# Hybrid encoder layer: VectorE held to the written order in the convolution stage, with its norm dealt out between matmul pieces

## The chip, the cores and the metric

The kernel runs on one core of a Trainium2 chip. The metric is the device time of one execution in microseconds (us); three runs of the kernel before gave 1720.52, 1720.84 and 1724.67, with a median of 1720.84. Profiles are of one execution each. The engines are TensorE (PE: matmuls, with PEld for its weight loads), VectorE (DVE), ScalarE (ACT), GpSimd (POOL) and SyncE (SP, which issues most transfers).

## What is computed

One layer of an encoder on a sequence of 1024 positions with width 1024, all in float32. The part that matters here is the token mixer:

```
h    = rmsnorm(x)
proj = h @ w_in                       # 1024 x 8192: glu (2x512), q, v, z_f, z_b, og, g_a, g_b
a    = glu(proj[glu])                 # 512 channels
a    = depthwise_conv(a, 31 taps) + b
a    = silu(layernorm(a) * ln_w + ln_b)
a    = a @ pw_w                       # 512 -> 1024
o    = bidirectional gated scan over q, v, z_f, z_b
y    = sigmoid(g_a) * a + sigmoid(g_b) * (norm(o) * silu(og)) @ o_w
x    = x + y @ w_out
```

A feed-forward block with a gated three-tap convolution and a last norm follow.

## The kernel before

**Layout.** Channels lie on the 128 partitions and positions along the free axis, in two halves of 512 (`H`). Every matrix product is made of 128 x 128 x 512 matmuls. For precision an operand is split into a high and a low part, and each product is three matmuls (`mm3`, lines 148 to 150). `split` (line 124) makes the parts: ScalarE casts the high part into its page, then VectorE subtracts it from the source and writes the low part.

**Pairs.** Most columns of the combined projection are made two column blocks at a time by `pair_job`, with Strassen's scheme in Winograd's form: seven products instead of eight, in the order 1, 2, 6, 7, 5, 4, 3. One product is twelve matmuls, in two pieces of six; a pair has 14 pieces, and there are 19 pairs (`NPAIRS`), so 266 pieces. Products 1, 6, 5 and 3 add up in one bank `mm` (the row bank), product 2 goes into `tr`, 7 and 4 into `sc`. Copies of a bank to SBUF are ScalarE's (line 440). VectorE evacuates three of the four quadrants through `store` (line 817): evac(0,0) after product 2, evac(1,1) after product 5, evac(1,0) after product 4; evac(0,1), after product 3, is ScalarE's. Product 3 adds into the row bank that evac(1,1) reads, so it waits for that evacuation.

The weights of a pair are three wide pages (1024 elements a partition) and a half one, each as high and low part: one for products 1 and 2 and one for 6 and 3 (both from the ring `wp`, four pages), one for 7 and 5 and the half page for 4 (ring `wq`, three pages). They are made from loaded rows (ring `wr`, two pages), a column page (`sw`) and a quadrant (`w4`). Sums of weight blocks come either from VectorE (`first`, pair 0 and from pair 14 on) or from accumulating transfers that GpSimd issues (line 301).

**Order.** `run_jobs` takes a job's pieces one by one and prepares the next job after `lead` pieces of the current one. `Weights` holds the preparation as steps with pauses in between; each piece advances it by one tick. Without `late` all steps of a pair are run at once when it is prepared. `Stream.fill(n)` issues n pieces, keeping fractions. TensorE's instructions keep the written order in the whole kernel (`tc.manual_schedule` with PE alone, at the top). The other engines' instructions are put in order by the compiler's scheduler, except those that `pin` ties behind what was written before them on their engine.

**The convolution stage.** `conv_steps` (lines 1042 to 1058) is four channel groups of 31 taps, one VectorE instruction of 128 x 1024 each (lines 1050 and 1053), 124 in all; after each, 1.67 pieces of the pairs are issued (`CONV_FILL`). A group's result is stored to the DRAM scratch `d_cv` in two halves. For each half of the positions the layer norm follows in lumps: load the four groups back, issue 6 pieces, sum them and have TensorE add over the partitions (`all_rows`, line 591, a product with ones), subtract the mean (line 1081), issue 6 pieces, squares on ScalarE, sums on VectorE, one-column products for the sum of squares (line 602), 1/sqrt on GpSimd, 5 pieces, spread over the partitions again, then scale, shift, silu, split, store to `d_ca`, 12 pieces. `s_pairs.drain()` issues the rest. The scan's stage follows, with the remaining projections as filler.

The feed-forward block, much later, runs pairs as well, with `late=True`, no `direct`, and `lead` 1.

Of the kernel before, what the change touches and what calls it, by code (L numbers as in the profile page):

```python
# [10 lines left out]
F32 = mybir.dt.float32  # L11
F32R = mybir.dt.float32r
I32 = mybir.dt.int32
U8 = mybir.dt.uint8
AF = mybir.ActivationFunctionType
ALU = mybir.AluOpType
AX = mybir.AxisListType

P = 128
FILL = 1.77  # L20
TAIL = ((1, 2), (1, 1), (2, 4), (2, 3))
CONV_FILL = 1.67
NPAIRS = 19
LN_FILL = 6
LN_LAST = 12
GLU_FIRST = 4
GLU_LEAD = 6
GLU_FILL = 2
# [3 lines left out]
H = 512  # L32
# [15 lines left out]
def tile_hybrid_encoder(  # L48
# [22 lines left out]
    nc = tc.nc  # L71
    PSUM = bass.MemoryType.PSUM
    V, A, G, T = nc.vector, nc.scalar, nc.gpsimd, nc.tensor

    S, D = x.shape[1], x.shape[2]
    ND = D // P
    CW = conv_dw_w.shape[2]
    CK = conv_dw_w.shape[1]
    NCW = CW // P
# [6 lines left out]
    cp = ctx.enter_context(tc.tile_pool(name="const", bufs=1))  # L86
# [7 lines left out]
    def nm(s):  # L94
        uid[0] += 1
        return f"{s}_{uid[0]}"
# [3 lines left out]
    def bank(tag):  # L100
        return ps.tile([P, H], F32, tag=tag, name=nm(tag), bufs=BANKS[tag])

    def page(pool, tag, bufs, dt=F32):
        return pool.tile([P, H], dt, tag=tag, name=nm(tag), bufs=bufs)

    def tmp():
        return page(mp, "tm", 4)
# [15 lines left out]
    def split(hi, lo, src, eng, late=False):  # L123
        parts = A.copy(hi, src), eng.tensor_tensor(lo, src, hi.bitcast(F32), op=ALU.subtract)  # L124
        if late:
            for i in parts:
                pin(i)
        return hi, lo
# [65 lines left out]
    def run_jobs(jobs, lead=0, prime=0, first=None):  # L194


        live = collections.deque(maxlen=3)

        jobs = jobs if isinstance(jobs, collections.deque) else collections.deque(jobs)
        ready = collections.deque()  # L200

        def prepare(n):
            while jobs and len(ready) < n:
                prep, run = jobs.popleft()
                ready.append((run, prep()))
                live.append(ready[-1][1])

        def tick():
            for w in live:
                if isinstance(w, Weights):  # L210
                    w.tick()
            advance_chores()

        prepare(max(prime, 1))
        if prime:
            yield
        while ready:
            run, w = ready.popleft()
            pieces = run(w)
            for _ in itertools.islice(pieces, lead if first is None else first):  # L220
                tick()
                yield
            first = None
            prepare(1)
            for _ in pieces:
                tick()
                yield
            prepare(1)
# [299 lines left out]
    def vec(key, i):  # L528
        name, o = vec_off[key]
        return vecs[name][:, o + i : o + i + 1]  # L530


    def scratch(name, *dims):
        if not dims:
            return dp.tile([P, H], F32, name=name)
        return [scratch(f"{name}_{i}", *dims[1:]) for i in range(dims[0])]

    d_h = scratch("d_h", ND // 2)
    d_c = scratch("d_c", ND // 2, 4)
    d_cv = scratch("d_cv", NCW, 2)  # L540
    d_ca = scratch("d_ca", NCW, 2, 2)
    d_a = scratch("d_a", ND, 2)
    d_ga = scratch("d_ga", ND, 2)
# [29 lines left out]
    def rstd_small(dst, ss, n, late=False):  # L573
        hold = pin if late else lambda i: i
        hold(G.tensor_scalar(dst, ss, 1.0 / n, EPS, op0=ALU.mult, op1=ALU.add))
        hold(G.tensor_tensor(dst, dst, mhalf.to_broadcast(list(dst.shape)), op=ALU.pow))

    def diagonals(r):

        tiny = [cp.tile([P, 4], F32R, name=nm("rp"), tag=tag, bufs=2) for tag in ("rh", "rl")]  # L580
        split(*tiny, r, V)
        pages = [page(mp, "tm", 4, F32R) for _ in range(2)]
        for d, t in zip(pages, tiny):
            for c in range(4):
                gain = t.bitcast(F32)[:, c : c + 1]
                A.activation(d[:, c * P : (c + 1) * P], ident, AF.Copy, scale=gain)
        return pages

    def all_rows(b, parts):
        for n, part in enumerate(parts):  # L590
            T.matmul(b, ones_r, part, start=n == 0, stop=n == len(parts) - 1)
        return b

    def spread(b, rs, diags):
        A.copy(rs, all_rows(b, diags))
        return rs

    def rstd_over_partitions(sq, n, tag, rs, early=False):

        b = bank(tag)  # L600
        for c in range(4):
            T.matmul(
                b[:, c : c + 1], sq[:, c * P : (c + 1) * P], ones_m[:, 0:1], start=True, stop=True
            )
        r = cp.tile([P, 4], F32, name=nm("r4"), tag="r4", bufs=2)
        V.tensor_copy(r, b[:, 0:4])
        rstd_small(r, r, n, early)
        if early:
            diag = tmp()
            pin(  # L610
                G.tensor_tensor(
                    diag.rearrange("p (c e) -> p c e", c=4),
                    view(ident, 0, [[0, 4], [1, P]]),
                    view(r, 0, [[1, 4], [0, P]]),
                    op=ALU.mult,
                )
            )
        else:
            diags = diagonals(r)
        yield  # L620
        b = bank(tag)
        if early:
            T.matmul(b, ones_m, diag, start=True, stop=True)
            pin(A.copy(rs, b))
            yield rs
        else:
            yield spread(b, rs, diags)
# [178 lines left out]
    gl = []  # L806
# [40 lines left out]
    def in_pair(n):  # L847
        (c0, e0), (c1, e1) = todo[2 * n], todo[2 * n + 1]
        evs = (e0, e1)
        return pair_job(  # L850
            in_cols(c0),
            in_cols(c1),
            NK2,
            lambda i: ht[i],
            p1,
            p1,
            lambda e, *quadrant: evs[e](*quadrant),
            first=n == 0 or n >= 14,
            columns=2,
        )  # L860

# [175 lines left out]

    jobs = collections.deque(in_pair(n) for n in range(1, NPAIRS))
    jobs.appendleft((lambda: w_pair0, pair0[1]))
    s_pairs = Stream(run_jobs(jobs, 4))  # L1040

    def conv_steps():
        for j in (3, 0, 1, 2):
            acc = p1.tile([P, S], F32, tag="ca", name=nm("acc"), bufs=2)
            g = gl[j]

            def tap(k):
                return vec("cdw", k * NCW + j)

            V.tensor_scalar(acc, g[:, 0:S], tap(0), vec("cb", j), op0=ALU.mult, op1=ALU.add)  # L1050
            yield
            for k in range(1, CK):
                V.scalar_tensor_tensor(  # L1053
                    acc, g[:, k : k + S], tap(k), acc, op0=ALU.mult, op1=ALU.add
                )
                yield
            for half in range(2):
                nc.sync.dma_start(d_cv[j][half], acc[:, half * H : (half + 1) * H])

    for _ in conv_steps():  # L1060
        s_pairs.fill(CONV_FILL)


    def total(ts, o):
        V.tensor_tensor(o, ts[0], ts[1], op=ALU.add)
        for t in ts[2:]:
            V.tensor_tensor(o, o, t, op=ALU.add)
        return o

    for half in range(2):  # L1070
        xs = []
        for j in range(NCW):
            if j % 2 == 0:
                both = p1.tile([P, 2, H], F32, tag="ca", name=nm("cx"), bufs=2)
            nc.sync.dma_start(both[:, j % 2, :], d_cv[j][half])
            xs.append(both[:, j % 2, :])
        s_pairs.fill(LN_FILL)
        sums = [page(mp, "tm", 4, F32R) for _ in range(2)]
        mean = all_rows(bank("ob"), split(*sums, total(xs, tmp()), V))
        for t in xs:  # L1080
            V.scalar_tensor_tensor(t, mean, -1.0 / CW, t, op0=ALU.mult, op1=ALU.add)
        s_pairs.fill(LN_FILL)
        sqs = [tmp() for _ in xs]
        for sq, t in zip(sqs, xs):
            A.activation(sq, t, AF.Square)
        rstd = rstd_over_partitions(total(sqs, sqs[0]), CW, "ob", tmp())
        next(rstd)
        s_pairs.fill(5)
        rs = next(rstd)
        for j, xn in enumerate(xs):  # L1090
            V.tensor_tensor(xn, xn, rs, op=ALU.mult)
            V.tensor_scalar(xn, xn, vec("lnw", j), vec("lnb", j), op0=ALU.mult, op1=ALU.add)
            A.activation(xn, xn, AF.Silu)
            both = gp0.tile([P, 2, H], F32R, tag="gl", name=nm("ch"), bufs=NCW)
            for dst, part in zip(d_ca[j][half], split(both[:, 0, :], both[:, 1, :], xn, V)):
                nc.sync.dma_start(dst, part.bitcast(F32))
        s_pairs.fill(LN_LAST)
    s_pairs.drain()
    p1.release()
    gp0.release()  # L1100

# [982 lines left out]
```

## Time and profile before

| | |
|---|---|
| median of three runs | 1720.84 us |
| the profiled execution | 1720.08 us |
| its span, first to last instruction | 1718.0 us |
| mean granted clock of TensorE | 0.998 |
| pairs on TensorE | from about 112 to 481 us |
| taps on VectorE | 80.3 to 316 us |
| layer norm's last silu (line 1093) begins | 471.5 us |

Times in a profile count from the span's start. A group row of the page gives line, engine, operation, output and inputs, shape and count, then the busy time in us and the mean of one instruction in ns, then the engine's idle time just before them and what ended it. A waits row gives the waiting engine and what it was about to do, the instruction waited for, the total in us, the count and the longest. In the timeline the columns are start and duration; `x4` means that four like instructions in a row are merged, and brackets hold the idle time before. A stretch row has the stretch and its length, busy time and count of PE, PEld, DVE, ACT and POOL, the granted clock, the busy share of the transfer engines and GB/s. Matmuls are pipelined, so two of them overlap in the timeline and a busy TensorE can still lose time.

### The profile page before, as it was taken

To read this page: it belongs to the slowest core of one execution; us is meant where nothing else is said; L and a number is where in the kernel's file an instruction comes from. 1 tells how busy PE (TensorE), PEld (TensorE's weight loads), DVE (VectorE), ACT (ScalarE), POOL (GpSimd) and SP (SyncE) were. 2 spreads that over 40 slices of the span, in tenths; PEclk is the share of its full clock that TensorE was granted. 3 is DMA by queue.
4 is the path that set the end of the run, shared out by engine and by line. 5 is a ranking of instruction groups with operands and counts; after the bars stand their busy time and mean duration, and the time that the engine had idled before them with its cause. 6 is when DMAs were issued, how large, how long until landed. Compare 5 with 4: busy or idle time off the path is not lost.

```text
span 1718.0 us, 30765 instructions
## 1 busy us (share of the span) xinstructions
PE 1697.2 (99%) x11902; PEld 1414.6 (82%) x11902; DVE 1262.1 (73%) x1938; ACT 829.0 (48%) x1561; POOL 241.6 (14%) x281
## 2 busy tenths in 40 slices
PE   8999999999999999999999999999999999999998
PEld 6788888888888888888888888888888888888787
DVE  5899999645778888888656467667777776657865
ACT  7444333334666777776441245444334433542334
POOL 2212222200001111111100002122222222000110
PEclk9999999999999999999999999999999999999999
DMA  7887788854673444436788455577778776773852
GB/s 243 276 213 182 186 190 202 199 158 147 214 251 99 138 128 134 127 116 202 228 280 273 123 172 178 148 161 153 164 167 174 172 174 151 235 264 100 213 97 99
DMA packets 335943, 306.18 MB, mean 178 GB/s; under 512 B 17454, under 2 KB 249014, under 8 KB 335798
## 3 DMA queue, kind: packets, MB, share of 16 engines
q1 hardware_dynamic: 288438, 265.42, 48.6%
q0 software_dynamic: 47360, 38.81, 15.4%
q8 instruction: 93, 1.52, 0.4%
q14 instruction: 52, 0.43, 0.1%
HBM read 201.40 MB, written 84.93 MB: 167 GB/s over the span
## 4 chain that ended last, share of the span: by engine, by line
PE 61%; DVE 1%; ACT 1%; issue 0%; DMA 0%; POOLq 0%; ACTq 0%; DVEq 0%
PE mm L148 14%; PE mm L150 14%; PE mm L149 14%; PE sc L148 3%; PE sc L150 3%; PE sc L149 3%; PE ob L1389 2%; PE tr L148 1%; PE tr L150 1%; PE tr L149 1%; PE sc L1211 1%; PE sc L1297 1%; PE mm L1348 1%; PE sc L1348 1%; PE ob L1211 0%
## 5 line engine op out<-in xcount | busy, mean ns | idle before, releaser
L148 PE MATMUL mm<-hx,wp 128*128 128x512 f32 x1068 | 426.3, 399 | 2.1 <-DVE ev L817 2.0
L150 PE MATMUL mm<-hx,wp 128*128 128x512 f32 x1068 | 416.8, 390 | 0.5 <-DVE wp L124 0.5
L149 PE MATMUL mm<-hx,wp 128*128 128x512 f32 x1068 | 416.5, 390 | 0.2 <-POOL hx L124 0.2
L124 ACT CAST wp<-wr 128x1024 fp32r<-128x1024 f32 (+2 forms) x147 | 147.3, 1002 | 212.0 <-PE mm L149 168.9
L148 PEld LDWEIGHTS mm<-hx,wp 128*128 128x128 f32 x1068 | 200.6, 188 | 45.2 <-DVE ev L817 4.6
L150 PEld LDWEIGHTS mm<-hx,wp 128*128 128x128 f32 x1068 | 200.5, 188 | 44.5 <-DVE wp L124 1.4
L149 PEld LDWEIGHTS mm<-hx,wp 128*128 128x128 f32 x1068 | 200.8, 188 | 39.0 <-POOL hx L124 0.6
L124 DVE TENSOR_TENSOR wp<-wr,wp 128x1024 fp32r<-128x1024 f32 (+2 forms) x145 | 169.6, 1170 | 35.8 <-ACT wp L124 29.7
L1053 DVE SCALAR_TENSOR_TENSOR acc<-gl,v_b,acc 128x1024 f32<-128x1024 f32 x120 | 148.9, 1278 | 0.3
L440 ACT COPY su<-mm 128x512 f32<-128x512 f32 x82 | 47.6, 581 | 79.9 <-PE mm L150 79.7
L1329 POOL DMA_DIRECT2D S<-D x64 | 36.3, 573 | 284.4 <-ACT jk L1394 128.7
L1158 DVE TENSOR_TENSOR qF<-qF,tb 128x512 f32<-128x512 f32 x96 | 65.8, 686 | 14.2 <-ACT A L1192 13.6
L124 ACT CAST wq<-sw 128x1024 fp32r<-128x1024 f32 x41 | 43.2, 1054 | 62.0 <-PE mm L149 35.1
L148 PE MATMUL tr<-hx,wp 128*128 128x512 f32 x180 | 70.1, 390 | 0.0
L150 PE MATMUL tr<-hx,wp 128*128 128x512 f32 x180 | 70.1, 389 | 0.0
L149 PE MATMUL tr<-hx,wp 128*128 128x512 f32 x180 | 70.0, 389 | 0.0
L1667 DVE SCALAR_TENSOR_TENSOR tm<-gp,v_a,tm 128x512 f32<-128x512 f32 x88 | 66.0, 750 | 4.0 <-ACT tm L1665 2.0
L1158 DVE TENSOR_TENSOR kG<-kG,tb 128x512 f32<-128x512 f32 x96 | 65.7, 687 | 4.4 <-ACT A L1192 2.6
L301 POOL DMA_DIRECT2D sw<-in_ffn_w_up_dram x38 | 49.8, 1501 | 117.8 <-DMA sw<-in_ffn_w_up_dram 85.9
L148 PE MATMUL sc<-hy,wq 128*128 128x512 f32 x164 | 64.2, 391 | 0.0
L150 PE MATMUL sc<-hy,wq 128*128 128x512 f32 x164 | 63.8, 389 | 0.0
L149 PE MATMUL sc<-hy,wq 128*128 128x512 f32 x164 | 63.8, 389 | 0.0
(381 smaller groups left out, 3731.3 us busy)
## 6 DMA issues: line engine op xcount, KB each, us to landing
wr<-in_w_in_dram SPq DMA_DIRECT2D x48, 512.0 KB, 6.2
wr<-in_ffn_w_up_dram SPq DMA_DIRECT2D x22, 512.0 KB, 5.4
sw<-in_w_in_dram SPq DMA_DIRECT2D x38, 256.0 KB, 3.8
d_g<-ft SPq DMA_DIRECT2D x38, 256.0 KB, 2.2
sw<-in_ffn_w_up_dram SPq DMA_DIRECT2D x38, 256.0 KB, 3.2
sw<-in_ffn_w_up_dram POOLq DMA_DIRECT2D x38, 256.0 KB, 6.5
wr<-sw POOLq DMA_DIRECT2D x32, 256.0 KB, 3.4
wr<-wr POOLq DMA_DIRECT2D x32, 256.0 KB, 3.2
```

Of the source, the lines that this page charges most:

```text
L124: parts = A.copy(hi, src), eng.tensor_tensor(lo, src, hi.bitcast(F32), op=ALU.subtract)
L148: T.matmul(acc, whi[:, k, :], ahi, start=first, stop=False, skip_group_check=again)
L149: T.matmul(acc, whi[:, k, :], alo, start=False, stop=False, skip_group_check=again)
L150: T.matmul(acc, wlo[:, k, :], ahi, start=False, stop=last, skip_group_check=again)
L301: G.dma_start(o, a, accum_op=ALU.add)
L440: A.copy(t, acc)
L1053: V.scalar_tensor_tensor(acc, g[:, k : k + S], tap(k), acc, op0=ALU.mult, op1=ALU.add)
L1158: return V.tensor_tensor(o, a, b, op=op)
L1329: G.dma_start(S_t[g : g + 32, :, g : g + 32], D_t[g : g + 32])
L1348: T.matmul(u[:, sl], kTs[d][:, sl], v[:, c, :], start=True, stop=True)
L1389: T.matmul(o[:, sl], l, r, start=(n == 0), stop=(n == len(terms) - 1))
L1667: V.scalar_tensor_tensor(c, g[:, o + k : o + k + H], vec("fdw", k * NF + j), c, op0=ALU.mult, op1=ALU.add,)
```

## The change

Inside the stage VectorE's instructions now keep the written order too. The pairs after the first stage their weight casts (`late`), with the next pair prepared after one piece instead of four, and pairs from 14 on use the branch `direct`, which was there but unused: sums on VectorE, the second operand loaded into the ring `wr`. Taps are followed by 1.6 pieces instead of 1.67. The four accumulators stay on chip: two in `ca`, two in slots of `gl` whose groups are done; `d_cv` is gone. The norm becomes a generator, `conv_norm`, that yields after nearly every step how many pieces to issue. The copies of the sums of squares and of the high parts are ScalarE's. A group's low part and its store follow one step after its scale, shift and silu. Sizes, products and results are the same.

```
-CONV_FILL = 1.67
+CONV_FILL = 1.6
-LN_FILL = 6
-LN_LAST = 12
...
-    d_cv = scratch("d_cv", NCW, 2)
...
-            first=n == 0 or n >= 14,
+            first=n == 0,
+            late=n > 0,
+            direct=n >= 14,
...
-    s_pairs = Stream(run_jobs(jobs, 4))
+    s_pairs = Stream(run_jobs(jobs, 1))
+
+    conv_order = (3, 0, 1, 2)
+    conv_out = []
 
     def conv_steps():
-        for j in (3, 0, 1, 2):
-            acc = p1.tile([P, S], F32, tag="ca", name=nm("acc"), bufs=2)
+        for n, j in enumerate(conv_order):
+            pool, tag, bufs = (p1, "ca", 2) if n < 2 else (gp0, "gl", NCW)
+            acc = pool.tile([P, S], F32, tag=tag, name=nm("acc"), bufs=bufs)
+            conv_out.append(acc)
...
-            for half in range(2):
-                nc.sync.dma_start(d_cv[j][half], acc[:, half * H : (half + 1) * H])
...
+    def conv_norm(half, pages):
+        xs = [t[:, half * H : (half + 1) * H] for t in conv_out]
+
+        def add(o, a, b):
+            V.tensor_tensor(o, a, b, op=ALU.add)
+
+        s = tmp()
+        add(s, xs[0], xs[1])
+        yield 1
+        add(s, s, xs[2])
+        yield 1
+        add(s, s, xs[3])
+        parts = [page(mp, "tm", 4, F32R) for _ in range(2)]
+        A.copy(parts[0], s)
+        yield 1
+        V.tensor_tensor(parts[1], s, parts[0].bitcast(F32), op=ALU.subtract)
+        yield 2
+        mean = all_rows(bank("ob"), parts)
+        yield 1
+        squares = []
         for t in xs:
             V.scalar_tensor_tensor(t, mean, -1.0 / CW, t, op0=ALU.mult, op1=ALU.add)
+            squares.append(tmp())
+            A.activation(squares[-1], t, AF.Square)
+            yield 1
+        for q in squares[1:]:
+            add(squares[0], squares[0], q)
+            yield 1
+        b = bank("ob")
+        for c in range(4):
+            T.matmul(b[:, c : c + 1], squares[0][:, c * P : (c + 1) * P], ones_m[:, 0:1], start=True, stop=True)
+        r = cp.tile([P, 4], F32, name=nm("r4"), tag="r4", bufs=2)
+        A.copy(r, b[:, 0:4])
+        rstd_small(r, r, CW)
+        yield 3
+        diags = diagonals(r)
+        yield 3
+        rs = spread(bank("ob"), tmp(), diags)
+        yield 1
+        for n in range(NCW + 1):
+            if n < NCW:
+                j, xn = conv_order[n], xs[n]
+                V.tensor_tensor(xn, xn, rs, op=ALU.mult)
+                V.tensor_scalar(xn, xn, vec("lnw", j), vec("lnb", j), op0=ALU.mult, op1=ALU.add)
+                A.activation(xn, xn, AF.Silu)
+                hi, lo = (pages[n % 2][:, i, :] for i in range(2))
+                A.copy(hi, xn)
+            if n > 0:
+                V.tensor_tensor(last[2], last[0], last[1].bitcast(F32), op=ALU.subtract)
+                for dst, part in zip(d_ca[conv_order[n - 1]][half], last[1:]):
+                    nc.sync.dma_start(dst, part.bitcast(F32))
+            last = (xn, hi, lo)
+            yield 3 if n < NCW else 0
+
+    with tc.manual_schedule(engines={mybir.EngineType.DVE}):
+        for _ in conv_steps():
+            s_pairs.fill(CONV_FILL)
+        split_pages = [gp0.tile([P, 2, H], F32R, tag="gl", name=nm("ch"), bufs=NCW) for _ in range(2)]
+        for half in range(2):
+            for pieces in conv_norm(half, split_pages):
+                s_pairs.fill(pieces)
+        s_pairs.drain()
```

More of the change, by code (lines that the diff above doesn't have):

```diff
@@ L1056, in conv_steps @@
                 yield
-            for half in range(2):
-                nc.sync.dma_start(d_cv[j][half], acc[:, half * H : (half + 1) * H])
[L1060 to L1079, printed above, removed]
+    def conv_norm(half, pages):
[16 more added lines that the diff above has]
+        squares = []
@@ L1080, in tile_hybrid_encoder @@
         for t in xs:
             V.scalar_tensor_tensor(t, mean, -1.0 / CW, t, op0=ALU.mult, op1=ALU.add)
[L1082 to L1096, printed above, removed]
@@ L1097, in tile_hybrid_encoder @@
-        s_pairs.fill(LN_LAST)
-    s_pairs.drain()
+            squares.append(tmp())
[6 more added lines that the diff above has]
+        for c in range(4):
+            T.matmul(
+                b[:, c : c + 1],
+                squares[0][:, c * P : (c + 1) * P],
+                ones_m[:, 0:1],
+                start=True,
+                stop=True,
+            )
```

## The prediction

> **What bounds the kernel now.** I read the page first (shares, costliest groups, DMA issues), then TensorE's waits while the pairs run, then busy times by stretch, then single instructions in the timeline.
>
> From the page (groups: count, then busy us and mean ns of one, then idle time before and who ended it):
>
> ```profile
> span 1718.0 us, 30765 instructions
> ...
> PE 1697.2 (99%) x11902; PEld 1414.6 (82%) x11902; DVE 1262.1 (73%) x1938; ACT 829.0 (48%) x1561; POOL 241.6 (14%) x281
> ...
> L124 ACT CAST wp<-wr 128x1024 fp32r<-128x1024 f32 (+2 forms) x147 | 147.3, 1002 | 212.0 <-PE mm L149 168.9
> ...
> L440 ACT COPY su<-mm 128x512 f32<-128x512 f32 x82 | 47.6, 581 | 79.9 <-PE mm L150 79.7
> ...
> wr<-sw POOLq DMA_DIRECT2D x32, 256.0 KB, 3.4
> wr<-wr POOLq DMA_DIRECT2D x32, 256.0 KB, 3.2
> ```
>
> TensorE is busy 99% of the span, so only what it loses in the stage can be won. The cast row will matter: the weight casts wait for TensorE (168.9 us in all), because the pages they write into are still being read.
>
> TensorE's waits from 112 to 480 us, where the nineteen pairs run, and the longest of them in the timeline (start, duration):
>
> ```profile
> PE mm L148 <- DVE ev L817: 2.0, 3, 0.9
> PE mm L148 <- ACT su L440: 0.5, 1, 0.5
> ```
>
> ```profile
> 186.84 0.39 PE L150 MATMUL sc<-hx,wq 128*128 128x512 f32 x1
> 188.11 0.50 PE L148 MATMUL mm<-hx,wp 128*128 128x512 f32 x1 [0.89 <-DVE ev L817]
> 188.45 0.39 PE L149 MATMUL mm<-hx,wp 128*128 128x512 f32 x1
> ```
>
> This is the step from product 4 (bank sc) to product 3, which goes on adding into a row bank that VectorE must have read for evac(1,1). Here is VectorE at that time:
>
> ```profile
> 183.06 0.81 DVE L1050 TENSOR_SCALAR acc<-gl,v_b,v_a 128x1024 f32<-128x1024 f32 x1 [2.41 <-DMA d_cv<-acc]
> 183.79 3.67 DVE L1053 SCALAR_TENSOR_TENSOR acc<-gl,v_b,acc 128x1024 f32<-128x1024 f32 x3
> 187.38 0.68 DVE L817 TENSOR_TENSOR ev<-su,mm 128x512 f32<-128x512 f32 x1
> ```
>
> It stood 2.41 us before a tap whose accumulator was still being stored, then did four taps, and only then the evacuation that TensorE needed. The idle time on TensorE's row is too small a measure, as matmuls overlap: 188.11 minus 186.84 is 1.27 us where one matmul is due. The loss is better read from counts. The stretches (TensorE, its weight loads, VectorE, ScalarE, GpSimd, each busy us and count):
>
> ```profile
> 112.00:304.00 192.00, 189.89 (x831) 155.28 (x830) 186.85 (x186) 75.86 (x106) 43.63 (x40) 1.00 0.80 184
> 304.00:480.00 176.00, 175.54 (x782) 145.06 (x781) 103.88 (x136) 74.40 (x120) 13.94 (x15) 1.00 0.65 190
> 1080.00:1480.00 400.00, 400.00 (x1767) 331.20 (x1766) 295.49 (x393) 170.15 (x243) 83.05 (x76) 1.00 0.73 167
> ```
>
> The last row is the feed-forward pairs: 400 us without an idle moment, 1767 matmuls, so 0.2264 us each, 1.36 us a piece of six. At that pace the 831 matmuls of the first row need 188.1 us: it loses 3.9. In the second, 16 of the 782 are the norm's one-column products; the other 766 need 173.4 us, and the rest, 2.6 us, is those 16 and the ScalarE wait, which I put at 0.7 (its 0.5 idle and the slow matmul behind it). So about **4.6 us** can be won here, 0.27% of the time; 0.3% is what a measurement of this kernel can tell from no change.
>
> The Trainium skill (Perfetto Trace Analysis, Identifying the Most-Contended Engine) would judge TensorE's headroom by the share of weight loads instead of by busy time. It would leave some 19% in the first row (155.28 of 192). The trace speaks against reading it so here: the row that loses nothing shows 331.20 of 400, 83%, as well.
>
> **The change part by part.**
>
> *Taps in program order.* The rows for VectorE's steps, spaced start to start:
>
> ```profile
> 104.12 4.87 DVE L1053 SCALAR_TENSOR_TENSOR acc<-gl,v_b,acc 128x1024 f32<-128x1024 f32 x4
> ```
>
> ```profile
> 404.29 1.22 DVE L124 TENSOR_TENSOR wp<-wr,wp 128x1024 fp32r<-128x1024 f32 x1
> 406.35 2.48 DVE L1081 SCALAR_TENSOR_TENSOR cx<-ob,cx 128x512 f32<-128x512 f32 x4 [0.84 <-PE ob L591]
> 408.75 1.22 DVE L124 TENSOR_TENSOR wp<-wr,wp 128x1024 fp32r<-128x1024 f32 x1
> 409.88 0.68 DVE L817 TENSOR_TENSOR ev<-tr,su 128x512 f32<-128x512 f32 x1
> 410.48 0.68 DVE L297 TENSOR_TENSOR wr<-wr,sw 128x512 f32<-128x512 f32 x1
> ```
>
> A tap takes 1.20 us of the engine (four in 4.87, the last one's tail overlapping), the low part of a 1024-wide page 1.13, a 512-wide step 0.60, a mean subtraction 0.62. A pair is 14 pieces, 19.0 us of TensorE. In it VectorE has 14/1.6 = 8.75 taps (10.5), three wide low parts and a half one (4.0), three evacuations (1.8): 16.3 us, 86%. The order is now piece by piece, so at evac(1,1) at most the few steps since product 5 began stand ahead, and it is due only two pieces (2.72 us) later. I expect the 3.9 us to go, and the 0.7 us too, as ScalarE gets squares one at a time. The feed-forward row supports it: there the pairs are staged in this same way (late, lead 1) and nothing waits, though with VectorE at 74% and not in order. VectorE's early start on the taps is lost:
>
> ```profile
> 80.30 0.81 DVE L1050 TENSOR_SCALAR acc<-gl,v_b,v_a 128x1024 f32<-128x1024 f32 x1
> ```
>
> It ran them from 80 us on, before the first pair; now the written order puts evac(0,0) of pair 0 before the fifth tap. That costs nothing, since 124 taps now spread over 198 pieces, 269 us, and the order follows TensorE anyway.
>
> *Results on chip.* Gone are sixteen transfers of 256 KB through d_cv and these idle times of VectorE:
>
> ```profile
> DVE acc L1050 <- DMA d_cv<-acc: 3.2, 2, 2.4
> DVE tm L1067 <- DMA cx<-d_cv: 3.1, 1, 3.1
> DVE tm L1065 <- DMA cx<-d_cv: 3.1, 2, 2.2
> ```
>
> The first is what stood before the late evacuation above, so its worth to TensorE is in the 3.9 us already. The other two fall where VectorE works 104 of 176 us and TensorE does not wait for it: worth nothing. SyncE's queue is shorter by those issues. GpSimd's accumulating transfers stay for pairs 1 to 13 and were already absent from 14 on; the additions there are the same, only the second operand's page moves from the ring sw to wr.
>
> *Staged casts from pair 14 on.* This is where the change costs. Pair n+1 is prepared after piece 1 of pair n; by the ticks, its first wide page (products 1, 2) is cast after piece 5, the column and row sums follow piece 11, the page for products 6 and 3 follows piece 12, that for 7 and 5 piece 13, the half page piece 3 of the next pair. The page for 6 and 3 lies in a ring of four pages of which the first two are already refilled, so it overwrites the page that product 3 of pair n reads until piece **14**. In program order VectorE stands still from piece 12 to 14 and then for ScalarE's cast of 1.00 us, which starts at once:
>
> ```profile
> 253.85 1.05 ACT L124 CAST wp<-wr 128x1024 fp32r<-128x1024 f32 x1 [1.91 <-PE tr L149]
> ```
>
> With the hand-over I take 1.1 us from the end of piece 14. Behind it queue evac(1,0), the low part after piece 13 and the norm's steps; and TensorE's order is fixed as well, so it waits where a norm matmul stands before they are done. The Trainium skill says of the hardware (PSUM — Partial Sum Buffer, Engine vs sequencer instructions) that VectorE's queue is a strict FIFO. The rows at 183.06 agree: 2.41 us before one tap, and the evacuation stayed behind it.
>
> *The dealt-out norm.* The taps end after piece 198 (124 x 1.6). Half 0 has its mean matmul after piece 203 and its sum-of-squares matmul after 211; half 1 after 235 and 243. Pairs end at 196, 210, 224, 238, 252, 266. From the rows:
>
> Mean, half 0, from the end of piece 196: cast 1.1, low part 1.13, evacuation 0.6, low part 1.13, the last two taps 2.4, add 0.6, half page 0.6, two adds 1.2 make 8.76. Then, with ScalarE's copy (0.58) beside it, evac(0,0) 0.6, a low part 1.13 and the subtraction 0.68 to its end: 11.2. TensorE is there after seven pieces, 9.5. It waits **1.7**. (The load of that low part can come late: the ring wr, two pages, now takes two loads a pair,
>
> ```profile
> wr<-in_w_in_dram SPq DMA_DIRECT2D x48, 512.0 KB, 6.2
> ```
>
> and if it starts when the page for 6 and 3 is split, at 2.2, it lands at 8.4 and is cast at 9.5; VectorE is there at 9.4. So at most a few tenths.)
>
> Squares, half 0, from the end of 210: 1.1, low part 1.13, add 0.6, evacuation 0.6, low part 1.13, add 0.6, add 0.68: 5.84. TensorE is there after one piece, 1.36. It waits **4.5**.
>
> Squares, half 1, from the end of 238: 1.1, low part 1.13, subtraction 0.62, evacuation 0.6, low part 1.13, three subtractions 1.86, add 0.6, half page 0.6, adds 0.6 and 0.68: 8.9. TensorE is there after five pieces, 6.8. It waits **2.1**.
>
> Mean, half 1: eleven pieces (14.9 us) after 224 with only some 11 us queued; none. The step from squares to spread took, in the kernel before,
>
> ```profile
> 414.33 0.95 PE L602 MATMUL ob<-ones_r,tm 128*128 128x1 f32 x8
> 422.09 0.62 PE L591 MATMUL ob<-tm,ones_r 128*128 128x512 f32 x2
> ```
>
> 7.8 us, and six pieces (8.2 us) now stand between: none. The normalising steps have no TensorE reader in the stage: none.
>
> Sum of the waits: **8.3 us**. The trace does not show such waits. Below they are bounded by the waits list above, which has no norm matmul: 0. Above, by one more cast (1.0) late in each of the three: 11.4. I take 8.3, as its terms are rows.
>
> Total: 8.3 - 4.6 = **+3.7 us**. The profiled execution took 1720.1 us with its span of 1718.0, which gives 1723.8; the median of the three runs is 1720.84, and on that I forecast **1724.5 us**, +0.2%: no change that can be told.
>
> **The rivals.**
>
> *The norm waits do not come* (chance 0.24): the order at the norm is looser than I read it, or VectorE is not held behind the page for 6 and 3. For it: in the waits list the norm, which came in lumps, cost TensorE nothing. Against it: the ring has four pages and each is read to the end of product 3. Then only the gain is left, 1720.84 - 4.6 = 1716.2. One part in eight of it finds a further 0.6 us and passes 0.3%.
>
> *VectorE falls behind in the tap stage* (0.12), which ends slower. For pairs 1 to 13 the page for 6 and 3 needs two accumulating transfers one after the other, 3.4 and 3.2 us. They start once the first page is split, some 0.9 us after piece 5, so with about 1 us of issue they land 8.5 us after it; the page is cast after piece 14, nine pieces or 12.2 us. If they are late by more than those 3.7 us, VectorE stands before the page with taps and evacuations behind it. It must make up for that from 19.0 - 16.3 = 2.7 us a pair. A rest of 0.5 us a pair on TensorE's path over thirteen pairs is 6.5 us: 1731. Against it, the feed-forward row, which runs these transfers without a wait of TensorE.
>
> *The change does not do what it says* (0.04): order and stage come out much as now, and the time stays near 1720.8.
>
> **How the numbers follow.** My forecast has 0.60. Within it the waits run from 5.5 (each a third shorter) to 11.4, so the time from 1721.7 to 1727.6; the line of 0.3% is 1726.0, and a quarter of it lies above. Slower by over 0.3%: 0.25 x 0.60 + 0.12, about 0.28. Faster by over 0.3%: 0.03. Within: 0.69. The range takes in the first rival and a part of the second: 1715.8 to 1729.
>
> **What would show it.** Right: no wait of TensorE on L817 between 112 and 300 us; 88 matmuls in each 20 us there; VectorE near 86%; new waits of TensorE on bank ob with VectorE as the releaser, the longest at a sum-of-squares matmul with a one-column result; VectorE idle until ScalarE's wp cast at the end of pairs 13 to 17. Wrong: no wait on ob (then the first rival), or waits of mm on L124 or L817 every 19 us (the second). If the evacuation waits stay, taps were not what made VectorE late.

## The result, and the profile after

The kernel after took 1752.63 us (median of 6 runs, 1750.58 to 1755.04), the kernel before in the same comparison 1720.68 us (6 runs, 1719.16 to 1724.67). The ratio is 1.0186, 95% interval 1.0174 to 1.0197: 32 us slower. The profiled execution took 1750.58 us with a span of 1748.5.

The main waits of TensorE between 112 and 520 us, where the kernel before had 2.5 us in all:

```profile
PE mm L146 <- DVE ev L814: 13.6, 8, 2.8
PE ob L1094 <- DVE tm L1068: 7.7, 2, 4.5
PE ob L588 <- DVE tm L1079: 2.5, 2, 2.3
```

The line numbers have moved: L146 to L148 are the three matmuls of `mm3`, L122 is `split`, L814 VectorE's evacuation, L817 now ScalarE's function behind it, L1057 the tap. Of the norm, L1068 is an addition, L1077 and L1079 make the high and low part of the sum, L1085 subtracts the mean, L588 and L1094 are its two matmul steps. The first row is the wait before product 3 that was to go; the other two are the norm's. The stretches that the prediction used, of the kernel after:

```profile
112.00:304.00 192.00, 179.60 (x775) 145.57 (x774) 149.27 (x148) 68.80 (x100) 39.79 (x37) 0.99 0.69 159
304.00:480.00 176.00, 165.42 (x715) 135.34 (x714) 137.40 (x152) 62.50 (x98) 17.15 (x18) 0.98 0.58 159
1080.00:1480.00 400.00, 400.00 (x1770) 330.76 (x1769) 292.67 (x387) 171.81 (x244) 91.89 (x87) 1.00 0.72 167
```

In the first stretch TensorE issues 775 matmuls where 831 stood before and 848 fit at full pace. VectorE is busy 149.27 of 192 us, 78%: less than the 86% of the prediction, and yet TensorE waits for it. The feed-forward pairs are as before.

Added up from the distances between matmul starts, TensorE loses 16.6 us against its pace from 112 to 395 us (3.8 before), 17.7 us from 395 to 520 us (1.6 before), and 17.1 us in all the rest (16.6 before). So there are two losses to explain, some 13 us in the tap stage and some 16 us around the norm; together they make 29 of the 30.5 us between the two spans.

**The tap stage.** VectorE around one evac(1,1), in the timeline:

```profile
161.28 0.68 DVE L814 TENSOR_TENSOR ev<-tr,su 128x512 f32<-128x512 f32 x1
163.65 1.22 DVE L122 TENSOR_TENSOR wp<-wr,wp 128x1024 fp32r<-128x1024 f32 x1 [1.69 <-ACT wp L122]
164.79 5.24 DVE L1057 SCALAR_TENSOR_TENSOR acc<-gl,v_b,acc 128x1024 f32<-128x1024 f32 x4
169.95 0.68 DVE L814 TENSOR_TENSOR ev<-su,mm 128x512 f32<-128x512 f32 x1
```

ScalarE over the same time:

```profile
162.05 0.63 ACT L817 ACTIVATE ev<-ev 128x512 f32<-128x512 f32 x1 [0.66 <-DVE ev L814]
162.58 1.04 ACT L122 CAST wp<-wr 128x1024 fp32r<-128x1024 f32 x1
...
170.67 0.63 ACT L817 ACTIVATE ev<-ev 128x512 f32<-128x512 f32 x1 [6.56 <-DVE ev L814]
171.20 1.03 ACT L122 CAST wq<-sw 128x1024 fp32r<-128x1024 f32 x1
```

TensorE at the end of it:

```profile
168.53 0.39 PE L148 MATMUL sc<-hx,wq 128*128 128x512 f32 x1
170.69 0.50 PE L146 MATMUL mm<-hx,wp 128*128 128x512 f32 x1 [1.77 <-DVE ev L814]
```

Read them in order of time. VectorE evacuates (0,0) at 161.28. ScalarE's Silu of that result follows at 162.05, and only then, at 162.58, the cast of the page, because `late` ties the cast (`pin`) behind what was written before it on ScalarE. VectorE's next instruction is the low part of that page; it stands 1.69 us with four taps and evac(1,1) behind it. TensorE then stands at product 3. At 170.67 the same starts again with the page for 7 and 5.

In all, from 112 to 300 us, VectorE waits this long for ScalarE's casts:

```profile
DVE wp L122 <- ACT wp L122: 23.6, 16, 2.4
DVE wq L122 <- ACT wq L122: 13.2, 8, 1.7
```

36.8 us, or 4.1 us for each of the nine pairs of that time. Not all of it is the Silu's: with the casts untied (e1 below) 13.3 us of such waits stay. And in the taps row at 164.79 four taps take 5.24: with 1.28 for one alone (the mean of all taps on the page) they start 1.32 us apart. The prediction's row at 104.12 gives 1.20 in the same way; there the scheduler alternated between two accumulators, here each tap adds into what the one before it wrote. Seven taps a pair in such rows make 0.8 us. So VectorE needs 16.3 + 4.1 + 0.8 = 21.2 us a pair, and TensorE offers 19.0. The wait at product 3 ended at 149.58 us in pair 1 and at 278.37 us in pair 7, six pairs apart: 21.5 us a pair, of which 0.3 are one run of slowed matmuls (last section).

**The norm.** TensorE at the sum of squares of half 0, and VectorE before it:

```profile
419.42 0.39 PE L148 MATMUL mm<-hx,wp 128*128 128x512 f32 x1
424.29 1.86 PE L1094 MATMUL ob<-ones_r,tm 128*128 128x1 f32 x8 [4.48 <-DVE tm L1068]
```

```profile
416.30 0.68 DVE L1085 SCALAR_TENSOR_TENSOR acc<-ob,acc 128x512 f32<-128x512 f32 x1
419.35 1.23 DVE L122 TENSOR_TENSOR wp<-wr,wp 128x1024 fp32r<-128x1024 f32 x1 [2.37 <-ACT wp L122]
420.49 0.68 DVE L1068 TENSOR_TENSOR tm<-tm,tm 128x512 f32<-128x512 f32 x1
421.09 0.68 DVE L814 TENSOR_TENSOR ev<-sc,su 128x512 f32<-128x512 f32 x1
421.69 1.21 DVE L122 TENSOR_TENSOR wq<-sw,wq 128x1024 fp32r<-128x1024 f32 x1
422.83 1.41 DVE L1068 TENSOR_TENSOR tm<-tm,tm 128x512 f32<-128x512 f32 x2
```

This is the queue that the prediction wrote out: cast, low part, addition, evacuation, low part, two additions, and then the matmul.

### The profile page after: what moved, and what is told of

It reads as the page before. It is cut to its first block, busy times and chain, and to the rows that moved or that the text cites. A ratio compares the mean times of both kernels' runs of the same rounds, so it can differ in the third digit from the quotient of the medians.

```text
span 1748.5 us, 30723 instructions
## 1 busy us (share of the span) xinstructions
PE 1706.4 (98%) x11902; PEld 1419.9 (81%) x11902; DVE 1268.1 (73%) x1936; ACT 826.3 (47%) x1563; POOL 241.3 (14%) x281
## 4 chain that ended last, share of the span: by engine, by line
PE 59%; DVE 1%; ACT 1%; DMA 1%; issue 1%; SPq 0%; POOLq 0%; ACTq 0%; DVEq 0%
PE mm L146 14%; PE mm L148 14%; PE mm L147 13%; PE sc L146 3%; PE sc L147 3%; PE sc L148 3%; PE ob L1422 2%; PE tr L146 1%; PE tr L147 1%; PE tr L148 1%; PE sc L1244 1%; PE mm L1381 1%; PE sc L1381 1%; PE sc L1330 0%; PE ob L1244 0%
## 5 line engine op out<-in xcount | busy, mean ns | idle before, releaser
L146 PE MATMUL mm<-hx,wp 128*128 128x512 f32 x1068 | 427.8, 401 | 13.6 <-DVE ev L814 13.6
L148 PE MATMUL mm<-hx,wp 128*128 128x512 f32 x1068 | 417.6, 391 | 0.5 <-DVE wp L122 0.5
L146 PEld LDWEIGHTS mm<-hx,wp 128*128 128x128 f32 x1068 | 201.2, 188 | 57.9 <-DVE ev L814 17.4
L122 ACT CAST wp<-wr 128x1024 fp32r<-128x1024 f32 (+2 forms) x147 | 147.1, 1001 | 213.8 <-PE mm L147 177.1
L148 PEld LDWEIGHTS mm<-hx,wp 128*128 128x128 f32 x1068 | 201.2, 188 | 44.8 <-DVE wp L122 1.4
L122 DVE TENSOR_TENSOR wp<-wr,wp 128x1024 fp32r<-128x1024 f32 (+2 forms) x145 | 169.7, 1170 | 80.9 <-ACT wp L122 79.3
L1057 DVE SCALAR_TENSOR_TENSOR acc<-gl,v_b,acc 128x1024 f32<-128x1024 f32 x120 | 153.7, 1281 | 2.0
L146 PE MATMUL tr<-hx,wp 128*128 128x512 f32 x180 | 70.6, 392 | 0.0
L148 PE MATMUL tr<-hx,wp 128*128 128x512 f32 x180 | 70.3, 390 | 0.0
L122 DVE TENSOR_TENSOR wq<-sw,wq 128x1024 fp32r<-128x1024 f32 x41 | 50.3, 1226 | 20.6 <-ACT wq L122 20.5
L148 PE MATMUL mm<-hy,wp 128*128 128x512 f32 x164 | 64.4, 393 | 0.2 <-DVE wp L122 0.2
L146 PE MATMUL sc<-hy,wq 128*128 128x512 f32 x164 | 64.5, 393 | 0.0
L147 PE MATMUL mm<-hy,wp 128*128 128x512 f32 x164 | 64.3, 392 | 0.0
```

What stands on the lines that cost most here:

```text
L146: T.matmul(acc, whi[:, k, :], ahi, start=first, stop=False, skip_group_check=again)
L147: T.matmul(acc, whi[:, k, :], alo, start=False, stop=False, skip_group_check=again)
L148: T.matmul(acc, wlo[:, k, :], ahi, start=False, stop=last, skip_group_check=again)
L1057: V.scalar_tensor_tensor(acc, g[:, k : k + S], tap(k), acc, op0=ALU.mult, op1=ALU.add)
```

## The experiments

Theory A: the tap stage is lost to the tied casts behind the Silu, under VectorE's written order. Theory B: it is lost to taps on one accumulator. For the norm, the prediction's own account, the page for 6 and 3, was to be tested. All kernels are the one after with the edit shown, unless the text says otherwise. Each ratio is to the kernel before, whose median was 1721.07 us beside e1 to e4, 1721.03 beside e5 to e8 and 1721.28 beside e9 and e10.

**e1, casts on ScalarE not tied.** VectorE's low parts stay tied.

```
-            for i in parts:
+            for i in parts[late == "lo":]:
                 pin(i)
...
-            late=n > 0,
+            late="lo" if n > 0 else False,
```

> The changed kernel, but in the convolution stage the ScalarE cast of a staged weight page is no longer tied behind what was written before it on ScalarE; VectorE's low part stays in the written order. Theory A (the tie puts each cast behind a Silu that waits for the evacuation just before it, so VectorE idles 1.6 to 1.7 us twice a pair and becomes the bound for pairs 0 to 8): the 13.6 us of TensorE's waits on the evacuation go, with the slow matmuls behind them some 17 us, to 1735 us. Rival B (taps that follow each other on one accumulator, 1.32 us apart instead of 1.20, overload VectorE): about 1752, unchanged. Rival C (the accumulating transfers are late): unchanged.

1730.83 us (4 runs), ratio 1.0054 (1.0037 to 1.0072). First stretch and waits from 112 to 520 us:

```profile
112.00:304.00 192.00, 192.00 (x849) 158.99 (x848) 166.24 (x162) 78.78 (x108) 44.74 (x42) 1.00 0.78 178
```

```profile
PE ob L1094 <- DVE tm L1068: 6.6, 2, 4.5
PE ob L588 <- DVE tm L1079: 1.4, 2, 1.2
PE ob L588 <- ACT tm L1077: 0.6, 1, 0.6
```

Full pace in the tap stage, with 849 matmuls, and VectorE at 86.6%, as the prediction had it. No wait on L814 is left. The cast now comes ahead of the Silu that it stood behind:

```profile
155.46 1.06 ACT L122 CAST wp<-wr 128x1024 fp32r<-128x1024 f32 x1 [1.91 <-PE tr L147]
157.28 0.63 ACT L817 ACTIVATE ev<-ev 128x512 f32<-128x512 f32 x1 [0.77 <-DVE ev L814]
```

Theory A holds; rival C of the expectation, late accumulating transfers, falls. What stays of VectorE's waits for casts, from 112 to 300 us, is

```profile
DVE wp L122 <- ACT wp L122: 13.1, 9, 2.4
```

and 0.2 us on wq. These nine waits, about one a pair, stand before the page for 6 and 3, whose cast waits until TensorE has finished product 3 (at 169.06 us, for one). They are some 1.4 us a pair: 16.3 + 0.8 + 1.4 = 18.5 us, which fits into 19.0. So 23.5 of the 36.8 us went with the tie, and the rest costs TensorE nothing. The run gained 4 us more than expected; the norm's waits, which shrank from 10.4 to 8.6 us, are a part of that, the rest was not traced.

**e2, taps alternating between two accumulators.**

```
-        for n, j in enumerate(conv_order):
...
+        for m in (0, 2):
...
+            for k in range(CK):
+                for j, g, acc in group:
```

> The changed kernel, but the taps alternate between two accumulators instead of finishing one group first. Theory A with B as its smaller part: six or seven taps a pair gain 0.12 us each, 0.8 of the 2.1 us that a pair loses, over eight pairs some 6 us: 1746. B alone: all of the tap stage's 17 us go, 1735. A alone or C: unchanged, 1752.

1747.90 us (4 runs), ratio 1.0157 (1.0141 to 1.0173). The taps are 1.20 us apart again, the waits on L814 fall from 13.6 to 10.4 us, the norm's stay. So B is real but the smaller part, some 5 us of the 32.

**e3, the page for 6 and 3 cast after the page for 7 and 5** (pairs from 14 on): after piece 14, up to which TensorE reads the page that it overwrites, and no longer after piece 12.

```
                 yield 1
-                w[6], w[3] = both(rows, None)
-                yield 1
                 w[7], w[5] = both(col, pool)
-                yield 4
+                yield 2
+                w[6], w[3] = both(rows, None)
+                yield 3
```

> The changed kernel, but from pair 14 on the page for products 7 and 5 is cast after piece 12 and that for 6 and 3 after piece 14, when its ring slot is free. Theory (VectorE stands before the page for 6 and 3 and holds the norm's steps): the waits of the sum-of-squares matmuls fall from 4.5 and 3.2 us to about 1.6 and 0, the slowed matmuls behind them go too, in all some 8 to 9 us: 1744. Rival (the norm's own steps are too late for the pieces between them): waits stay, 1752.

1745.50 us (4 runs), ratio 1.0140 (1.0125 to 1.0155). The norm's one-column matmuls wait 5.2 us instead of 7.7, those with the sums 0.9 instead of 2.5. The last pair's wait on L814 (1.4 us at 510 us) is gone as well. More was expected to go at the squares. VectorE there, in e3:

```profile
412.09 0.69 DVE L814 TENSOR_TENSOR ev<-su,mm 128x512 f32<-128x512 f32 x1 [2.29 <-issue]
...
415.28 0.68 DVE L1085 SCALAR_TENSOR_TENSOR acc<-ob,acc 128x512 f32<-128x512 f32 x1
417.60 1.23 DVE L122 TENSOR_TENSOR wq<-sw,wq 128x1024 fp32r<-128x1024 f32 x1 [1.64 <-ACT wq L122]
```

The fourth subtraction still stands behind evac(1,1) and the sums, and now the tied cast of the other page holds the additions up: on ScalarE it begins at 416.54 us, behind the square at 416.00 that waited for that subtraction. The page for 6 and 3 was a part of the cause, not all of it.

**e4, the scheduler's order on VectorE,** all else of the change kept.

```
-    with tc.manual_schedule(engines={mybir.EngineType.DVE}):
+    with ExitStack():
```

> The changed kernel without the written order on VectorE (staged casts, 1.6 pieces, dealt-out norm and on-chip results all kept). Theory (the order is what turns each late operand into idle time): taps fill the holes, evacuation waits fall below 4 us and the norm's waits below 3, about 1725. Rival (staging and ties on ScalarE cost by themselves): above 1745.

1716.89 us (7 runs), ratio 0.9974 (0.9963 to 0.9985): 4.2 us faster than before, and 8 us better than expected.

```profile
112.00:304.00 192.00, 192.00 (x848) 158.97 (x847) 191.03 (x190) 74.83 (x107) 44.09 (x41) 1.00 0.78 178
304.00:480.00 176.00, 176.00 (x785) 145.70 (x784) 101.56 (x133) 75.30 (x124) 13.25 (x15) 1.00 0.61 179
```

No wait of TensorE is left from 112 to 520 us. VectorE is busy 191 of 192 us in the first stretch, with the ties still there:

```profile
156.43 0.68 DVE L814 TENSOR_TENSOR ev<-tr,su 128x512 f32<-128x512 f32 x1
157.03 2.47 DVE L1057 SCALAR_TENSOR_TENSOR acc<-gl,v_b,acc 128x1024 f32<-128x1024 f32 x2
159.42 1.22 DVE L122 TENSOR_TENSOR wp<-wr,wp 128x1024 fp32r<-128x1024 f32 x1
```

```profile
157.20 0.63 ACT L817 ACTIVATE ev<-ev 128x512 f32<-128x512 f32 x1 [2.60 <-issue]
157.74 1.03 ACT L122 CAST wp<-wr 128x1024 fp32r<-128x1024 f32 x1
```

ScalarE's order is the same, Silu and then cast. But two taps fill VectorE's time until the cast is done, where the rows of the kernel after show 1.69 us of nothing. It takes the tie and the written order together to lose that time.

**e5, without the Silu.** The ties stay; the stores of q and the output gate leave the function out, so that nothing of ScalarE's lies between VectorE's evacuation and the cast.

```
-            (OFF_Q + h * DK, store(d_q[h], AF.Silu)),
-            (OFF_OG + h * DK, store(d_og[h], AF.Silu)),
+            (OFF_Q + h * DK, store(d_q[h])),
+            (OFF_OG + h * DK, store(d_og[h])),
```

> The changed kernel with its ties as they are, but the stores of pairs 0 to 7 leave out the Silu on q and on the out gate. Theory A (a tied cast is late because a Silu that waits for the evacuation stands before it): the tap stage's 17 us go as they did when the tie was taken away, to some 1732 us, with TensorE's waits on the evacuation under 1 us. Rival (the tie costs whatever stands before the cast): 1752.

1736.44 us (4 runs), ratio 1.0087 (1.0073 to 1.0100). The first stretch is at full pace (849 matmuls), the norm waits 7.7 and 2.5 us as in the kernel after. That is theory A's second leg: the tie costs because a function that waits for VectorE stands ahead. It also says why, in the kernel after, the waits in the tap stage end at pair 8, from which on the pairs (v and the z gates) store without a function.

**e6, a repaired order:** untied casts, alternating taps, the page for 6 and 3 later, and two more pieces ahead of the squares' matmul.

```
             add(squares[0], squares[0], q)
             yield 1
+        yield 2
         b = bank("ob")
```

> VectorE in the written order, with three repairs together (casts not tied on ScalarE, taps alternating between two accumulators, the page for 6 and 3 after piece 14) and two more pieces between the last sum of squares and its matmul. Theory (the written order costs only where something late stands before something due): the 17 us of the tap stage and most of the norm's 12 us go, to 1719 with waits of TensorE under 3 us in the stage. Rival (a fixed order on VectorE loses several us by itself): 1728 or more.

1721.31 us (11 runs), ratio 1.0000 (0.9991 to 1.0009). The stage itself loses nothing. But the four added pieces end the norm later (its last silu begins at 476.2 us, in e9 below at 471.4), ScalarE's first step of the scan begins at 488.21 us (in e9 at 484.06), and two matmuls of the scan wait for a copy by ScalarE. TensorE's waits from 480 to 520 us:

```profile
PE sc L1246 <- ACT A L1227: 1.9, 2, 1.0
```

**e7, the staging alone,** and **e8, the norm alone.** e7 is the kernel before with only `late`, `direct` and `lead` 1; e8 is the kernel before with only the dealt-out norm, the results on chip and 1.6 pieces; both in the scheduler's order.

```
-            first=n == 0 or n >= 14,
+            first=n == 0,
+            late=n > 0,
+            direct=n >= 14,
...
-    s_pairs = Stream(run_jobs(jobs, 4))
+    s_pairs = Stream(run_jobs(jobs, 1))
```

> The kernel before with only the staged casts (late from pair 1 on, direct from 14 on, next pair prepared after one piece); order by the scheduler, norm in lumps through the DRAM scratch. If the gain of 4 us that the scheduler's order showed comes from the staging: 1717. If it comes from the norm and the results on chip: 1721, as before.

> The kernel before with only the dealt-out norm, the results on chip and 1.6 pieces a tap; pairs prepared as before, order by the scheduler. If the gain of 4 us comes from here: 1717. If from the staging: 1720 to 1721, since only the wait on the accumulator's store (1.0 us) and the ScalarE wait (0.7) go.

e7: 1720.31 us (11 runs), ratio 0.9996 (0.9987 to 1.0005). e8: 1719.08 us (11 runs), 0.9986 (0.9977 to 0.9995). What is left in e7:

```profile
183.44 0.81 DVE L1052 TENSOR_SCALAR acc<-gl,v_b,v_a 128x1024 f32<-128x1024 f32 x1 [2.04 <-DMA d_cv<-acc]
184.17 2.47 DVE L1055 SCALAR_TENSOR_TENSOR acc<-gl,v_b,acc 128x1024 f32<-128x1024 f32 x2
186.56 0.68 DVE L817 TENSOR_TENSOR ev<-su,mm 128x512 f32<-128x512 f32 x1
```

The store of the accumulator still holds VectorE up, with 3.1 us of waits of TensorE behind two such places. In e8 that is gone and 1.7 us of other small waits are left. Neither half alone reaches the 1717 us that either expectation would have it reach. The two differences, 0.7 and 1.9 us, add up to less than the 4.2 us that e4 gains with both, but each is known to some 1.5 us only, so whether the halves help each other is not shown.

**e9 and e10, the added pieces taken back from the normalising steps;** e10 without the alternating taps.

```
-            yield 3 if n < NCW else 0
+            yield (3, 3, 2, 2, 0)[n]
```

> As the three repairs together, but the two pieces added ahead of the sum-of-squares matmul are taken from the normalising steps, so that the norm ends four pieces earlier. Theory (in that run the stage itself lost nothing, and the norm's later end pushed the scan's first inputs back, 1.9 us of waits and a slow run of matmuls of 1.4): the waits at the scan's start go, 1717 to 1718. Rival (the scan starts late because of the order kept on VectorE): 1721, unchanged.

> The same, but the taps finish one group before the next, as the change has them (1.32 us apart in a row). Theory (with the casts untied VectorE has 2 us a pair in hand, so 0.8 us a pair of slower taps hides): within 1 us of the alternating version, no wait on the evacuation. Rival (slower taps still make the evacuation late): 3 us or more slower than it.

e9: 1717.83 us (8 runs), ratio 0.9976 (0.9965 to 0.9988). e10: 1717.23 us (6 runs), 0.9971 (0.9959 to 0.9982). The first stretch of e10:

```profile
112.00:304.00 192.00, 192.00 (x848) 158.97 (x847) 166.19 (x164) 78.56 (x108) 44.44 (x41) 1.00 0.78 178
```

The slower taps on one accumulator cost nothing once the casts are untied: VectorE has room for their 0.8 us a pair and the 1.4 us of waits that stay, not for 4.9. The waits at the scan's start are gone in both, so what e6 lost there came from the pieces and not from the order on VectorE. e4, e9 and e10 are faster than the kernel before by 0.24 to 0.29%, and their intervals overlap.

## Why the prediction was wrong, point by point

- **The sum of a pair in the tap stage failed.** "16.3 us, 86%" counted VectorE's busy time and took its order as free of idle time. In program order it stood 4.1 us a pair before low parts whose cast was late, 23.5 of 36.8 us by the tie behind the Silu (e1), and the taps took 0.8 us more than priced. The 2.7 us of room were overdrawn by 2.2; instead of a gain of 3.9 us came a loss of 12.8. Untying the casts (e1), taking the Silu away (e5) or leaving the order to the scheduler (e4) each brought the stage back to full pace.
- **The second rival's end came, by another mechanism.** VectorE did fall behind in the tap stage, and TensorE did wait in each of the pairs 1 to 7. The rival looked for accumulating transfers that come late. VectorE's wait was for ScalarE's casts, and ScalarE's, as the rows at 162.05 and 162.58 show, for the Silu ahead. The prediction priced the cast itself (1.0 us) at the norm alone and never asked what `pin` puts ahead of it.
- **"The feed-forward row supports it" was the wrong support.** It has the same ties without the written order on VectorE, which is e4, not the kernel after. The prediction said "not in order" itself and drew nothing from it.
- **That the 4.6 us can be won was right,** but only where the ties cost VectorE no time: e4 gains 4.2 us, e10 4.1, each known to some 2 us.
- **The norm's waits came in their places:** mean of half 0, 2.3 us (1.7 said), squares of half 0, 4.5 (4.5), squares of half 1, 3.2 (2.1), mean of half 1, 0.2 (none); 10.2 in all for 8.3. e3 shows that the page for 6 and 3 was behind four tenths of it (with ScalarE's 0.2, 10.4 went to 6.3). Not foreseen were the clock after them (below), some 3.5 us, and the last pair's evacuation behind the norm's end, 1.6 us.
- **The first rival, no norm waits,** fell: they are in every run that keeps the written order unrepaired. The third, no change, fell too.
- **The signs to look for** served: 88 matmuls in 20 us (81 came) and VectorE near 86% were both missed, and the falsifier of evacuation waits that stay spoke: taps were not the main thing that made VectorE late, though e2 shows that their spacing had a part. The signs at the norm came true: waits on bank ob, the longest at a one-column matmul, behind a late cast into wp.

## What to carry to other kernels

When an engine is put into written order, add up its idle time as well as its busy time: for each instruction that needs another engine's result, follow that engine's queue back to what stands ahead there, and ask whether that in turn waits for the first engine. A tie that cost nothing while the scheduler filled the gap (e4) cost VectorE the whole gap once the order was written down. And pieces added ahead of a step push back what comes next (e6), so take them from a place that has too many (e9).

## What the runs showed of the hardware

After some waits TensorE's clock was halved. In the kernel after, the stretch behind the 4.48 us wait (the granted clock stands third from the end):

```profile
425.00:430.50 5.50, 5.50 (x17) 4.53 (x17) 0.18 (x1) 2.62 (x8) 1.23 (x2) 0.50 0.39 117
```

And two waits of the tap stage, in the timeline:

```profile
210.14 0.39 PE L148 MATMUL sc<-hx,wq 128*128 128x512 f32 x1
212.98 0.50 PE L146 MATMUL mm<-hx,wp 128*128 128x512 f32 x1 [2.45 <-DVE ev L814]
213.32 0.40 PE L147 MATMUL mm<-hx,wp 128*128 128x512 f32 x1
...
235.71 0.62 PE L146 MATMUL mm<-hx,wp 128*128 128x512 f32 x1 [2.82 <-DVE ev L814]
236.13 0.63 PE L147 MATMUL mm<-hx,wp 128*128 128x512 f32 x1
236.55 0.63 PE L148 MATMUL mm<-hx,wp 128*128 128x512 f32 x1
```

After 2.82 us of idle time the matmuls start 0.42 us apart instead of 0.23, for eight matmuls; after 2.45 us they do not. Behind the waits of 4.48 and 3.24 us nine and eight were slow. Each such run costs 0.2 us a matmul, some 1.6 us, on top of the wait. Over all the runs there was no sharp bound: one idle time of 1.84 us (e7) had eight slow matmuls behind it and one of 2.1 (e1) seven, one of 2.3 (in the kernel after) none. The Trainium skill (TensorE: Matmul & The Clock Gate, HAM oscillation) warns of idle gaps above some 3.4 us. The traces agree that the clock falls after such gaps, but show it after shorter ones as well.

The other surprise was the tap: 1.32 us from start to start when each adds into the accumulator that the one before it wrote, 1.20 when two accumulators alternate, on 128 x 1024 elements. What makes the 0.12 us was not separated.
